# Two norm factors of the last layer's boundary, taken from four sums per token gathered during the output projection

## The chip, the cores and the metric

The kernel runs on one core of a Trainium2 chip. The metric is the device time of one execution in microseconds (us); each kernel is timed in several runs and the median is given. PE is the matmul engine (TensorE), PEld its weight load, DVE the vector engine, ACT the scalar engine, POOL the general engine (GpSimd), SP the engine whose queue issues the DMAs.

## The reference

A sequence of 512 tokens with 1024 features goes through two hybrid layers and then two transformer layers with a context stream. All arithmetic is float32 in its result. The place that matters here is the middle of the last layer, between its attention and its feed-forward part:

```python
def rms_norm_2(x, g):
    xf = x.astype(jnp.float32)
    y = xf * lax.rsqrt(jnp.mean(xf * xf, axis=-1, keepdims=True) + EPS)
    return (y * g.astype(jnp.float32)).astype(x.dtype)
...
        y = ... @ w_out                          # attention, output projection
        x = x + g1 * rms_norm_2(y, norm_g[l, 1])         # first norm: of y
        h = rms_norm_2(x, norm_g[l, 2]) * (1.0 + sc2) + sh2   # second norm: of the new x
        x = x + g2 * rms_norm_2(swiglu(h, ffn_w_in[l], ffn_w_out[l]), norm_g[l, 3])
```

The first norm needs one factor per token, r1 = (mean(y^2) + eps)^-1/2. The second needs r2 = (mean(x'^2) + eps)^-1/2, where x' = x + G*y*r1 and G is the product of the gate g1 and the gain, one number per feature.

## The kernel before

Activations lie feature by feature: a tensor of 1024 features and 512 tokens is eight tiles of 128 partitions (features) by 512 columns (tokens), numbered k or f from 0 to 7. A sum over features is therefore a sum over tiles, and then a matmul with a column of ones (`ones_col`). Every matmul of a weight with an activation is done in three parts on values split in a high and a low half (`hh`, `hl` for the activation, `wh`, `wl` for the weight): high by high, high by low, low by high. The split of a weight tile is a cast on ACT (`weights`, L422) and a subtraction on POOL or, for one weight in three, on DVE (`lo`, L398 and L400). A weight has three buffers for the raw data and two for each half.

The last layer's second stretch runs so:

1. `out_proj` (L970): half of the output projection (features 0 to 3 of its input) was done earlier, beside the attention. Now the other four are added: for each of the eight output tiles f, `dense` loads a weight of 128x512, splits it, and runs 12 matmuls of 512 columns into one PSUM bank (four banks, tags "d" and "b", in turn); `proj` (L616 to L632) adds the bank to y on DVE (L625), ACT squares the sum (L503), and POOL adds the square to a running tile (L631; the last tile's square stays apart). Woven with it, `prepare` loads and splits four weights of the feed-forward part (`u0` to `u3`).
2. `boundary` (L579): the tile of squares and the last square go through the matmul with ones (`rstd_cols`, L389), then a small DVE operation (L481), the power -1/2 on POOL (L483), and four PE transposes that spread the factor over 128 partitions (`spread`, L498). Then `postnorm_tile` for each k: a DVE operation with G and r1 (L576) and an addition to x on POOL (even k) or DVE (odd k, L577). Then the new x is squared tile by tile on ACT (L503), the squares are added on DVE (L515, L518), and the same column sum, power and transposes give r2. Then `norm_tile` for each k (DVE L554, ACT L556 or L560) and the split of h (L557, L398).
3. `outer` runs the first four feed-forward weights, 12 matmuls for each tile k of h, into four banks. After that `ffn` goes on as a plain row of matmuls to the end of the kernel, and a last `boundary` writes the output.

The old x is loaded by two DMAs of 1 MB (L586) and the new x is written back by two (L593), on SP's queue.

The order of instructions on each engine is set when the program is built: a scheduler takes, by a number of priority that follows the order of the code, whatever is ready by its own reckoning. `ahead(n)` shifts that number. In this stretch `stage(low=3, load=800, split=-200, ...)` holds: loads of weights stand 800 places earlier, and splits of weights (ACT cast and POOL or DVE subtraction) 200 places later than where the code has them. On the chip each engine then works strictly in the order written.

Of the kernel before, what the change touches and what calls it, by code (L numbers as in the profile page):

```python
# [11 lines left out]
F32 = mybir.dt.float32  # L12
# [4 lines left out]
AF = mybir.ActivationFunctionType  # L17
ALU = mybir.AluOpType
# [4 lines left out]
D = 1024  # L23
KD = D // 128
S = 512
NT = S // 128
# [3 lines left out]
EPS = 1e-6  # L30
# [169 lines left out]
class Net:  # L200
# [136 lines left out]
    def first(self, g, n):  # L337
        for _ in range(n):
            next(g)
            yield  # L340
# [235 lines left out]
        nc.vector.scalar_tensor_tensor(t, y[k // 4][:, k % 4, :], gain[:, k:k + 1], r, op0=ALU.mult, op1=ALU.mult)  # L576
        (nc.vector if k in [1, 3, 5, 7] else nc.gpsimd).tensor_add(x[:, k, :], x[:, k, :], t)  # L577

    def boundary(self, y, ysq, xsrc, gain, nxt, xdst, early=None):  # L579


        nc = self.nc
        with self.phase("x") as ph:
            x = ph.tile([128, KD, S], F32, name=self.name("x"))
            for i in range(2):
                nc.sync.dma_start(x[:, 4 * i:4 * i + 4], xsrc[:, 4 * i:4 * i + 4])  # L586
            al = partial(self.tl, ph, dt=F32, tag="bp", bufs=8 if early else 5), self.bank if early else self.flat
            yield
            if y is not None:
                yield from self.postnorm_steps(x, y, ysq, S, gain, al)  # L590
            if xdst is not None:
                for i in range(2):
                    nc.sync.dma_start(xdst[:, 4 * i:4 * i + 4], x[:, 4 * i:4 * i + 4])  # L593
            yield
            if nxt is None:
                return None
            h = yield from self.prenorm_steps(x, S, *nxt, al=al)
            if not early:
                return h
            acc = [self.bank([128, S], "d") for _ in range(2)]  # L600
            for _ in range((len(early) - 1) // 2):
                w = self.wide()
                acc += [w[:, 0, :], w[:, 1, :]]
            acc = acc[:len(early)]
            self.outer(early, h, acc)
            yield
            return h, dict(enumerate(acc))

    def outer(self, ws, h, acc, ks=range(KD)):

# [1159 lines left out]
    def run(self):  # L1770
        nc, I = self.nc, self.I
        x1, x2, x3, x4 = (self.scr([128, KD, S], f"x{i}") for i in range(4))
        self.stage(low=3)
        h, ready = self.start()
# [3 lines left out]
        m, mc = (self.mods2(0, ada[0][0][i], "xy"[i]) for i in range(2))  # L1778
        with self.phase("c1") as self.c1:
# [10 lines left out]
            with self.phase("ctx") as ph:  # L1790
                done = {}
                with self.phase("xc") as px:
                    xc = px.tile([128, KD, CL], F32, name="xc0")
                    nc.sync.dma_start(xc, I["ctx"])
                    y, sq = self.weave((self.out_proj(I["w_out"][0], mix[0], S, *mix[1:]), 8, 0),
                                       (self.keep(done, self.prenorm_steps(xc, CL, *mc(0), pool=ph)), 9, 0))
                scc, win, lat = self.even_project(done["result"], CL, 0, False, ph)
                h = self.weave((self.boundary(y, sq, I["x"], self.post_mod1(0), self.pre_mod1(1), x1), 18, 0), (win(), 4.5, -200))
# [9 lines left out]
        with self.phase("c2") as self.c2:  # L1808
# [6 lines left out]
            with self.phase("ctxa") as ph:  # L1815
                at = self.area(ph, "c", kp=1, k=4, q=8, v=3, p=8)
                y, sq = self.weave((self.out_proj(I["w_out"][1], mix[0], S, *mix[1:]), 8, 30),
                                   (self.chain(self.even_ctx_window(at, scc["q"], oc[0]),
                                               self.even_latent(at, scc, CL, CL, oc[1])), 12, 0))
            self.stage(low=3)  # L1820
            with self.phase("ctxo") as ph:
                hc = self.split_o(oc, CL, self.new_h(CL, ph))
                done = {}
                h = self.weave((self.boundary(y, sq, x1, self.post_mod1(1), m(0), x2), 18, 0),
                               (self.keep(done, self.out_proj(I["ev_w_out"], hc, CL)), 8, 0))
# [13 lines left out]
            with self.phase("cf") as cf:  # L1839
# [14 lines left out]
                y, sq = self.result(self.out_proj(I["ev_w_out"], self.split_o(o, S, self.new_h(S)), S))  # L1854
                h = self.weave((self.boundary(y, sq, x2, m(1), m(2), x3), 18, 60), (rest, 14.4, 0))
            g2 = m(3)
            self.stage(low=3)
            m, mc = (self.mods2(1, ada[1][0][i], "xy"[i]) for i in range(2))
            with self.phase("ctx") as cx:
                with self.phase("ffn") as ph:  # L1860
# [3 lines left out]
                    f = self.ffn(0, h, S, hid)  # L1864
# [3 lines left out]
                    y, sq = self.weave((f, 8, 0), (self.keep(done, self.prenorm_steps(xc, CL, *mc(0), pool=cx)), 9, 0))  # L1868
                _, val, diff, keys, _ = self.odd_project(done["result"], CL, 0, False, cx)
                h = self.weave((self.boundary(y, sq, x3, g2, m(0), x4), 18, 0),  # L1870
                               (self.chain(diff(0), keys(), val(0), diff(1), val(1)), 5, 0))
        self.stage(low=3, max=-200, turn=300)
        with self.phase("odd") as ph:
# [4 lines left out]
            ready = {}  # L1878
# [9 lines left out]
            h = self.new_h(S)  # L1888
            self.split_o(o, S, h, range(4))
            y = self.open_y()  # L1890
# [5 lines left out]
        with self.phase("early") as ph:  # L1896
            early = []

            def prepare():
                for u in range(4):  # L1900
                    src = I["ffn_w_in"][1, u % 2 * NFH + u // 2].rearrange("p k c -> p (k c)")
                    early.append(self.weights(src, 1024, (ph, f"u{u}")))
                    yield

            y, sq = self.weave((self.out_proj(I["od_w_out"], h, S, y, range(4)), 8, 0),
                               (prepare(), 4.2, 0))
            h, ready = self.weave((self.boundary(y, sq, x4, m(1), m(2), x1, early), 1, 0))
            self.close_y()
            self.stage(low=3)
            with self.phase("ffn") as ph:  # L1910
                hid = lambda: [self.tl(ph, [128, KD, S], F32R, "hid", 2) for _ in range(2)]
                y, sq = self.result(self.ffn(1, h, S, hid, ready))
# [70 lines left out]
```

## Time and profile before

| | us |
|---|---|
| median of 3 runs | 2823.11 (2820.75 to 2828.60) |
| profiled execution, its own time | 2819.89 |
| span of its profile | 2818.1 |
| PE busy in the span | 2455.0 (87%) |
| DVE, ACT, POOL busy | 1258.7, 1188.2, 1079.4 |
| output projection's second half, last matmul | from 2383.5 to 2412.3 |
| first matmul of the feed-forward part | 2436.16 |
| last matmul of the feed-forward part | 2800.0 |

Times of rows are counted from the span's start. The share of PE is an average over many stages; the change touches one of them, between about 2384 and 2461 us. A row of the time line gives start, duration, engine, line of the code, operation, the tile written and the tiles read, the shape, and how many instructions it merges; in square brackets stands how long the engine was idle before and what ended that.

### The profile page before, as it was taken

How to read it: one execution, taken by the hardware profiler on the slowest of the kernel's cores; microseconds unless marked ns; L12 is line 12 of the kernel's file. 1: busy time of each engine (PE TensorE's matmuls, PEld its weight loads, DVE VectorE, ACT ScalarE, POOL GpSimd, SP SyncE). 2: the span in 40 equal slices, each digit the busy share in tenths (PEclk: the TensorE clock that was granted, in tenths of full speed). 3: DMA queues.
4: the chain of work that ended last, by engine and by line, in shares of the span. 5: the costliest groups of instructions: out<-in, count | busy, mean ns of one | idle time of the engine just before them, and what ended most of it. 6: DMA issues, size and time to landing. Idle time of an engine off the chain costs nothing. (4 is left out here: it accounts for less than half of the span.)

```text
span 2818.1 us, 35394 instructions
## 1 busy us (share of the span) xinstructions
PE 2455.0 (87%) x13052; PEld 1994.9 (71%) x13052; DVE 1258.7 (45%) x2065; ACT 1188.2 (42%) x2227; POOL 1079.4 (38%) x754
## 2 busy tenths in 40 slices
PE   6988896778888886769999899999888989799997
PEld 4765666666666665648998777777776777688886
DVE  3655357235646644445442631212645767421212
ACT  3534365333547534445554522222434646332222
POOL 2435235344533551213455732322542222443334
PEclk9988998888979987879999999999988989899998
DMA  7364644344344652335553545454444253333332
GB/s 244 121 205 156 207 165 154 107 140 162 104 124 139 213 182 100 116 112 143 174 159 135 186 135 172 149 169 133 148 140 158 90 153 113 113 100 97 94 97 75
DMA packets 170816, 400.56 MB, mean 142 GB/s; under 512 B 19378, under 2 KB 60820, under 8 KB 167316
## 3 DMA queue, kind: packets, MB, share of 16 engines
q1 hardware_dynamic: 170644, 398.31, 43.7%
q8 instruction: 103, 1.69, 0.2%
q14 instruction: 69, 0.57, 0.1%
HBM read 339.85 MB, written 58.39 MB: 141 GB/s over the span
## 5 line engine op out<-in xcount | busy, mean ns | idle before, releaser
L398 POOL TENSOR_TENSOR wl<-wr,wh 128x1024 fp32r<-128x1024 f32 (+3 forms) x245 | 538.2, 2198 | 899.5 <-ACT wh L422 451.5
L422 ACT CAST wh<-wr 128x1024 fp32r<-128x1024 f32 (+3 forms) x367 | 353.8, 964 | 706.5 <-PE d L389 279.5
L389 PE MATMUL d<-hh,wh 128*128 128x512 f32 x960 | 398.4, 415 | 19.7 <-ACT hh L556 7.8
L389 PE MATMUL d<-hl,wh 128*128 128x512 f32 x960 | 394.0, 410 | 1.9 <-DVE hl L557 0.9
L389 PE MATMUL d<-hh,wl 128*128 128x512 f32 x960 | 263.5, 403 | 0.0
L400 DVE SCALAR_TENSOR_TENSOR wl<-wr,wh 128x1024 fp32r<-128x1024 f32 (+3 forms) x122 | 152.1, 1246 | 227.8 <-PE d L389 91.9
L389 PEld LDWEIGHTS d<-hh,wh 128*128 128x128 f32 x960 | 190.6, 199 | 62.2 <-ACT hh L556 8.4
L389 PEld LDWEIGHTS d<-hl,wh 128*128 128x128 f32 x960 | 189.7, 198 | 42.5 <-issue 2.5
L389 PEld LDWEIGHTS d<-hh,wl 128*128 128x128 f32 x960 | 185.0, 195 | 39.6 <-issue 1.6
L400 DVE SCALAR_TENSOR_TENSOR pg<-b,pg 128x512 fp32r<-128x512 f32 (+1 forms) x208 | 137.2, 665 | 68.7 <-ACT pg L404 67.2
L389 PE MATMUL b<-hh,wh 128*128 128x512 f32 x416 | 164.2, 395 | 0.0
L389 PE MATMUL b<-hl,wh 128*128 128x512 f32 x416 | 163.2, 392 | 0.0
L934 POOL TENSOR_TENSOR oy<-pg,pg 64x256 f32<-64x256 f32 (+1 forms) x72 | 57.7, 802 | 262.3 <-DVE pg L932 91.3
L404 ACT CAST pg<-b 128x512 fp32r<-128x512 f32 (+1 forms) x208 | 117.1, 570 | 80.2 <-PE b L909 68.2
L882 DVE TENSOR_REDUCE sm<-s 128x1 f32<-128x768 f32 (+3 forms) x144 | 120.7, 846 | 26.6 <-PE s L389 25.9
L389 PE MATMUL d<-hc,wh 128*128 128x256 f32 x656 | 105.4, 311 | 23.7 <-DVE rp L400 11.8
L950 DVE SCALAR_TENSOR_TENSOR rp<-rp,d 128x512 f32<-128x512 f32 (+1 forms) x77 | 46.7, 607 | 165.5 <-ACT rp L949 165.4
L1745 DVE SCALAR_TENSOR_TENSOR rp<-rp,b 128x512 f32<-128x512 f32 (+1 forms) x64 | 38.1, 595 | 175.3 <-PE b L389 174.8
L389 PE MATMUL d<-hid,wh 128*128 128x512 f32 (+1 forms) x528 | 114.7, 361 | 1.5 <-POOL hid L398 1.5
L389 PEld LDWEIGHTS d<-hc,wh 128*128 128x128 f32 x656 | 94.9, 211 | 28.3 <-ACT wh L422 12.2
L389 PE MATMUL b<-hid,wh 128*128 128x512 f32 (+1 forms) x528 | 110.8, 361 | 0.0
L389 PE MATMUL b<-hh,wl 128*128 128x512 f32 x416 | 103.8, 389 | 0.0
(416 smaller groups left out, 5143.2 us busy)
## 6 DMA issues: line engine op xcount, KB each, us to landing
wr<-in_ffn_w_in SPq DMA_DIRECT2D x132, 512.0 KB
mr<-in_ada_w SPq DMA_DIRECT2D x96, 512.0 KB
wr<-in_ffn_w_out SPq DMA_DIRECT2D x48, 512.0 KB
x<-x SPq DMA_DIRECT2D x20, 1024.0 KB
wr<-in_w_in SPq DMA_DIRECT2D x38, 512.0 KB
mr<-in_w_mod SPq DMA_DIRECT2D x32, 512.0 KB
wr<-in_ev_w_in SPq DMA_DIRECT2D x20, 512.0 KB
wr<-in_ffn_w_out SPq DMA_DIRECT2D x24, 384.0 KB
```

Source lines behind the costliest of these rows:

```text
L389: self.nc.tensor.matmul(out, lhsT, rhs, start=start, stop=stop)
L398: self.nc.gpsimd.tensor_sub(out, src, hi)
L400: self.nc.vector.scalar_tensor_tensor(out, src, scale, hi, op0=ALU.mult, op1=ALU.subtract)
L404: self.nc.scalar.copy(hi, src)
L422: nc.scalar.copy(hi[:, :n], raw[:, :n])
L882: nc.vector.reduce_max(c, s, axis=AX.X, negate=True)
L934: nc.gpsimd.tensor_tensor(d, sel(t), sel(rs), op=ALU.mult)
L950: nc.vector.scalar_tensor_tensor(t, t, 1.0, ps, op0=ALU.add, op1=ALU.mult)
L1745: nc.vector.scalar_tensor_tensor(g, g, 0.5, pu, op0=ALU.mult, op1=ALU.mult)
```

## The change

The old x is loaded before the projection (`residual`). During the projection (`joint_proj`) four sums per token are gathered: of y^2, of (G*y)^2, of G*y*x and of x^2. With r1 known, the sum of squares of the new x is r1^2 * sum((Gy)^2) + 2 * r1 * sum(Gyx) + sum(x^2), so r2 follows from six small DVE operations on 128x4 numbers (`joint_boundary`) without a pass over the new x. For tiles 0 to 5 the terms are added tile by tile (squares of y and of Gy on POOL, Gyx and x^2 on DVE); tiles 6 and 7 go straight into the matmul with ones, for the squares with a two-column right side (1 and G^2). The column sums are matmuls on PE into one bank. In `joint_boundary` r1 and r2 are both spread at once, and for each k the new x, the normed h and the matmuls of `outer` follow each other. The new x is written after k = 3 and k = 7. `boundary` loses its `early` branch; its other callers do as before.

```diff
--- before.py
+++ after.py
@@ -576,15 +576,14 @@
         nc.vector.scalar_tensor_tensor(t, y[k // 4][:, k % 4, :], gain[:, k:k + 1], r, op0=ALU.mult, op1=ALU.mult)
         (nc.vector if k in [1, 3, 5, 7] else nc.gpsimd).tensor_add(x[:, k, :], x[:, k, :], t)
-    def boundary(self, y, ysq, xsrc, gain, nxt, xdst, early=None):
-
+    def boundary(self, y, ysq, xsrc, gain, nxt, xdst):
         nc = self.nc
         with self.phase("x") as ph:
             x = ph.tile([128, KD, S], F32, name=self.name("x"))
             for i in range(2):
                 nc.sync.dma_start(x[:, 4 * i:4 * i + 4], xsrc[:, 4 * i:4 * i + 4])
-            al = partial(self.tl, ph, dt=F32, tag="bp", bufs=8 if early else 5), self.bank if early else self.flat
+            al = partial(self.tl, ph, dt=F32, tag="bp", bufs=5), self.flat
             yield
             if y is not None:
                 yield from self.postnorm_steps(x, y, ysq, S, gain, al)
@@ -595,16 +594,109 @@
             if nxt is None:
                 return None
             h = yield from self.prenorm_steps(x, S, *nxt, al=al)
-            if not early:
-                return h
-            acc = [self.bank([128, S], "d") for _ in range(2)]
-            for _ in range((len(early) - 1) // 2):
-                w = self.wide()
-                acc += [w[:, 0, :], w[:, 1, :]]
-            acc = acc[:len(early)]
-            self.outer(early, h, acc)
-            yield
-            return h, dict(enumerate(acc))
+            return h
+    @contextmanager
+    def residual(self, xsrc):
+        with self.phase("x") as ph:
+            x = ph.tile([128, KD, S], F32, name=self.name("x"))
+            for i in range(2):
+                self.nc.sync.dma_start(x[:, 4 * i:4 * i + 4], xsrc[:, 4 * i:4 * i + 4])
+            yield x, (partial(self.tl, ph, dt=F32, tag="bp", bufs=8), self.bank)
+    def joint_proj(self, wsrc, h, y, ks, x, gain, al):
+        nc = self.nc
+        cols = self.flat([128, NT, 4])
+        w2 = self.sm([128, 2, 2])
+        nc.vector.memset(w2, 1.0)
+        nc.vector.tensor_tensor(w2[:, :, 1], gain[:, 6:8], gain[:, 6:8], op=ALU.mult)
+        n = [0]
+        def add(tile, rhs, c, last=False):
+            for t in range(NT):
+                self.mm(cols[:, t, c:c + rhs.shape[-1]], tile[:, t * 128:t * 128 + 128], rhs, n[0] == 0,
+                        last and t == NT - 1)
+                n[0] += 1
+        sums, late = None, []
+        for f in range(KD):
+            ps = self.dense(wsrc[f, :, ks[0]:ks[-1] + 1].rearrange("p k c -> p (k c)"), h, S, ks, "db"[f % 2])
+            dst = y[f // 4][:, f % 4, :]
+            new = al[0] if f == 0 else self.rp
+            g = gain[:, f:f + 1]
+            nc.vector.tensor_add(dst, ps, dst)
+            sq, xz = new([128, S]), new([128, S])
+            nc.scalar.activation(sq, dst, AF.Square)
+            nc.vector.scalar_tensor_tensor(xz, dst, g, x[:, f, :], op0=ALU.mult, op1=ALU.mult)
+            if f < 6:
+                z = new([128, S])
+                nc.scalar.activation(z, dst, AF.Square, scale=g)
+                if f == 0:
+                    sums = sq, z, xz
+                    xx = al[0]([128, S])
+                    nc.scalar.activation(xx, x[:, 0, :], AF.Square)
+                else:
+                    nc.gpsimd.tensor_add(sums[0], sums[0], sq)
+                    nc.gpsimd.tensor_add(sums[1], sums[1], z)
+                    nc.vector.tensor_add(sums[2], sums[2], xz)
+            else:
+                late.append((sq, xz))
+            for k in ((), (1,), (2,), (3,), (4,), (5,), (6, 7), ())[f]:
+                t = self.square(x[:, k, :], S)
+                nc.vector.tensor_add(xx, xx, t)
+            if f == 6:
+                for i, t in enumerate(sums):
+                    add(t, self.ones_col, i)
+            yield
+        add(xx, self.ones_col, 3)
+        for i, (sq, xz) in enumerate(late):
+            add(sq, w2[:, i, :], 0)
+            add(xz, self.ones_col, 2, i == 1)
+        return cols
+    def joint_boundary(self, y, cols, x, al, gain, nxt, xdst, early):
+        nc = self.nc
+        def power(ms):
+            r = self.sm([128, NT, 1])
+            nc.gpsimd.tensor_tensor(r, ms, self.mhalf[:, None, :].to_broadcast([128, NT, 1]), op=ALU.pow)
+            return r
+        ms, q = self.sm([128, NT, 1]), self.sm([128, NT, 1])
+        nc.vector.tensor_scalar(ms, cols[:, :, 0:1], 1.0 / D, EPS, op0=ALU.mult, op1=ALU.add)
+        r1 = power(ms)
+        ms = self.sm([128, NT, 1])
+        nc.vector.tensor_tensor(q, cols[:, :, 1:2], r1, op=ALU.mult)
+        nc.vector.scalar_tensor_tensor(q, cols[:, :, 2:3], 2.0, q, op0=ALU.mult, op1=ALU.add)
+        nc.vector.tensor_tensor(q, q, r1, op=ALU.mult)
+        nc.vector.tensor_tensor(q, cols[:, :, 3:4], q, op=ALU.add)
+        nc.vector.tensor_scalar(q, q, 0.0, None, op0=ALU.max)
+        nc.vector.tensor_scalar(ms, q, 1.0 / D, EPS, op0=ALU.mult, op1=ALU.add)
+        r2 = power(ms)
+        r1, r2 = self.spread(r1, S, al=al), self.spread(r2, S, al=al)
+        h = self.new_h(S)
+        acc = [self.bank([128, S], "d") for _ in range(2)]
+        w = self.wide()
+        acc += [w[:, 0, :], w[:, 1, :]]
+        def first(k):
+            t = al[0]([128, S])
+            nc.vector.scalar_tensor_tensor(t, y[k // 4][:, k % 4, :], gain[:, k:k + 1], r1, op0=ALU.mult, op1=ALU.mult)
+            (nc.gpsimd if k in [2, 4, 6] else nc.vector).tensor_add(x[:, k, :], x[:, k, :], t)
+        first(0)
+        for k in range(KD):
+            if k + 1 < KD:
+                first(k + 1)
+            self.norm_tile(h, x, k, S, r2, *nxt, al)
+            self.outer(early, h, acc, [k])
+            if k % 4 == 3:
+                nc.sync.dma_start(xdst[:, k - 3:k + 1], x[:, k - 3:k + 1])
+        return h, dict(enumerate(acc))
     def outer(self, ws, h, acc, ks=range(KD)):
@@ -1902,9 +1994,10 @@
                     early.append(self.weights(src, 1024, (ph, f"u{u}")))
                     yield
-            y, sq = self.weave((self.out_proj(I["od_w_out"], h, S, y, range(4)), 8, 0),
-                               (prepare(), 4.2, 0))
-            h, ready = self.weave((self.boundary(y, sq, x4, m(1), m(2), x1, early), 1, 0))
+            with self.residual(x4) as (x, al):
+                cols = self.weave((self.joint_proj(I["od_w_out"], h, y, range(4, 8), x, m(1), al), 8, 0),
+                                  (prepare(), 4.2, 0))
+                h, ready = self.joint_boundary(y, cols, x, al, m(1), m(2), x1, early)
             self.close_y()
             self.stage(low=3)
             with self.phase("ffn") as ph:
```

## Rows read from the trace of the kernel before

**Rows 1.** Busy time by stretch: us, then each engine's busy time, clock, DMA.
```profile
core 0: us, PE busy (x) PEld busy (x) DVE busy (x) ACT busy (x) POOL busy (x), PEclk, DMA share, GB/s
2400.00:2414.00 14.00, 13.06 (x62) 10.62 (x60) 6.73 (x7) 8.52 (x12) 13.75 (x10) 1.00 0.61 181
2420.00:2435.00 15.00, 2.96 (x12) 2.50 (x12) 10.60 (x18) 4.32 (x8) 5.70 (x4) 0.50 0.34 140
2435.00:2450.00 15.00, 13.84 (x51) 11.03 (x52) 8.82 (x12) 7.92 (x12) 5.21 (x4) 0.81 0.00 0
2740.00:2760.00 20.00, 20.00 (x90) 16.57 (x89) 3.81 (x5) 5.72 (x7) 9.09 (x5) 1.00 0.26 75
```

**Rows 2.** Time line of PE from 2384 to 2442 us.
```profile
2384.76 0.40 PE L389 MATMUL d<-hl,wh 128*128 128x512 f32 x1
...
2390.82 0.63 PE L389 MATMUL b<-hl,wh 128*128 128x512 f32 x1
...
2411.27 1.07 PE L389 MATMUL b<-hh,wl 128*128 128x512 f32 x4
2413.28 1.95 PE L389 MATMUL b<-blk,rp 128*128 128x1 f32 x16 [0.94 <-POOL rp L631]
...
2430.26 1.84 PE L389 MATMUL b<-blk,bp 128*128 128x1 f32 x8 [12.70 <-DVE bp L518]
2433.45 1.12 PE L498 MATMUL b<-ident,sm 128*128 128x128 f32 x4 [1.35 <-POOL sm L483]
2436.16 0.79 PE L389 MATMUL d<-hh,u0h 128*128 128x512 f32 x1 [1.60 <-ACT hh L556]
```

**Rows 3.** Time line of DVE, from the projection's end to the second norm.
```profile
2410.27 1.82 DVE L400 SCALAR_TENSOR_TENSOR wl<-wr,wh 128x1024 fp32r<-128x1024 f32 x1
2412.38 0.69 DVE L625 TENSOR_TENSOR y<-b,y 128x512 f32<-128x512 f32 x1 [0.29 <-PE b L389]
2415.26 0.16 DVE L481 TENSOR_SCALAR sm<-b 128x4 f32<-128x4 f32 x1 [2.19 <-PE b L389]
2417.60 2.06 DVE L576 SCALAR_TENSOR_TENSOR bp<-oy,x,b 128x512 f32<-128x512 f32 x3 [2.17 <-PE b L498]
2419.58 0.68 DVE L577 TENSOR_TENSOR x<-x,bp 128x512 f32<-128x512 f32 x1
...
2425.70 3.69 DVE L515 TENSOR_TENSOR bp<-bp,bp 128x512 f32<-128x512 f32 x6
...
2434.60 2.06 DVE L554 SCALAR_TENSOR_TENSOR bp<-x,x,b 128x512 f32<-128x512 f32 x3 [2.31 <-PE b L498]
```

**Rows 4.** Time line of ACT: the last square of y, the first tile of h.
```profile
2413.10 0.63 ACT L503 ACTIVATE rp<-y 128x512 f32<-128x512 f32 x1 [0.46 <-DVE y L625]
...
2435.39 0.72 ACT L556 ACTIVATE hh<-bp,ada 128x512 fp32r<-128x512 f32 x1 [8.46 <-DVE bp L554]
```

**Rows 5.** Time line of POOL in the projection and the first norm.
```profile
2395.29 2.55 POOL L398 TENSOR_TENSOR wl<-wr,wh 128x512 fp32r<-128x512 f32 x2 [5.86 <-PE b L389]
2397.79 1.29 POOL L631 TENSOR_TENSOR rp<-rp,rp 128x512 f32<-128x512 f32 x1
...
2403.88 2.13 POOL L631 TENSOR_TENSOR rp<-rp,rp 128x512 f32<-128x512 f32 x1
...
2409.73 3.50 POOL L631 TENSOR_TENSOR rp<-rp,rp 128x512 f32<-128x512 f32 x2
...
2415.50 1.02 POOL L483 TENSOR_TENSOR sm<-sm,mhalf 128x4 f32<-128x4 f32 x1
2418.42 2.96 POOL L577 TENSOR_TENSOR x<-x,bp 128x512 f32<-128x512 f32 x2 [1.90 <-DVE bp L576]
```

**Rows 6.** SP's queue: the new x is written, the next load of x.
```profile
2422.25 3.92 SPq L593 DMA_DIRECT2D x<-x  x2
2460.40 0.80 SPq L586 DMA_DIRECT2D x<-x  x2
```

## The prediction

> **What bounds the kernel now.** I read the table of busy time by stretch first. From the feed-forward part on, PE is busy in 20.00 of 20 us at the full clock (one slice of it stands in [rows 1], the others are like it). So whatever moves the first feed-forward matmul moves the end of the kernel by the same amount, and the question is only when that matmul starts. The same table shows two different stretches ahead of it. From 2400 to 2414 us, the output projection, PE has 13.06 of 14 us and POOL 13.75: both are full, DVE has half its time free. From 2420 to 2435 us PE has 2.96 of 15 us and its clock has fallen to 0.50, the lower level of 1.2 GHz: that is the boundary, where DVE and small steps bound it.
>
> The time line of PE gives the marks [rows 2]. The last projection matmuls start at 2411.27 and end at 2412.3. The column sum of squares is done at 2413.28 + 1.95 = 2415.23; I call this moment C. The first feed-forward matmul starts at 2436.16, so C to there is 20.93 us. Between lie eight new tiles of x, the second pass of squares that ends with six DVE additions of 3.69 us [rows 3], its own column sum of 1.84 us and transposes of 1.12 us [rows 2].
>
> **What the change takes off behind C.** After it, C is the moment when all four sums stand, and then follow, each waiting for the one before: a small DVE operation, 0.03 us of handing over and 0.16 [rows 3]; the power on POOL, 0.08 + 1.02 [rows 5]; six small DVE operations; a second power, 1.10; four transposes, 0.05 + 1.12 [rows 2]; the first normed tile on DVE, 0.03 + 0.74 (three take 2.06 when queued) [rows 3]; ACT, 0.05 + 0.72 [rows 4]; PE, 0.05. The six are shown nowhere as a chain. Six times 0.16 is 0.96, with 0.09 of gap each 1.5; I take 1.25, near the lower because that row is the same size. Sum: 0.19 + 1.10 + 1.25 + 1.10 + 1.17 + 0.77 + 0.77 + 0.05 = 6.4 us. The r1 spread is beside it. Behind it DVE makes two tiles of new x, 0.69 + 0.68 each, so it can be up to 0.6 us late for the normed tile. I take 6.7, bounds 6.3 and 7.3. Gain: 20.93 - 6.7 = 14.2 us.
>
> Behind the first matmul nothing new becomes the bound. Per pair of tiles DVE then has two operations of 0.69 with r1, two with r2, one addition and one split, about 4.2 us, while PE takes 24 matmuls; 90 take 20.00 us at full clock [rows 1], so 24 take 5.3. PE starts at the lower clock as it does now (0.79 and 0.63 a matmul, clock 0.81 over that stretch) [rows 1, 2]; I count no change there. The two writes of x move from 2422 to some 2440 and 2450; behind them on SP's queue stands first the load of 2460.40 [rows 6], so they delay nothing. The loads of the old x only stand earlier in the code; they still wait for their space, and I count nothing (bounds 0 and 1 us).
>
> **What it costs before C.** First PE. Four sums over eight tiles (three running tiles, the x^2 tile, two times two late ones) replace two, and 16 column-sum instructions for two tiles took 1.95 us, 0.98 a tile [rows 2]; at the lower clock it is 1.84. Were PE alone the limit, the projection would end where it does and C would be 2412.3 + 8 x 0.98 = 2420.1, 4.9 us later than now.
>
> Then POOL and DVE. Now POOL does one split and one addition a tile. For tiles 1 to 5 it gets a second addition, and DVE three operations that it has not now, all reading two tiles of SBUF: the product with x, its addition, the addition of x^2. The rows show that such a DVE operation and a POOL operation never run together. POOL's addition at 2409.73 is followed at once by another, 3.50 us for two where two splits took 2.55 [rows 5]; the DVE split that came in at 2410.27 and lasted 1.82 [rows 3] first stood until POOL's first was done (about 2411.0) and then held up the second for 1.1. In the first norm POOL's operation began at 2418.42 and is over at 2419.7 by the usual 1.29; the DVE addition of 2419.58 ends at 2420.26, 0.55 later, and POOL's pair lasts 2.96 instead of 2.55 [rows 3, 5]. So one share has to be split: POOL 1.25 (2.55 / 2 less the overlap of issuing) for an operation of 512 columns, DVE 0.55.
>
> From 2395.29, when POOL's first free weight buffer lets it start [rows 5], up to the last addition on POOL (of tile 5), that share must hold: on POOL five splits and ten additions, 15 x 1.25 = 18.75; on DVE six products, five additions of them and five of x^2, 16 x 0.55 = 8.8. Together 27.55, so 2422.8. A weight split on DVE in this stretch (1.1) and two of the x^2 additions done before it starts (2 x 0.55) cancel. Then PE still has seven tiles of sums to run, 7 x 0.98 = 6.9, beside which the last projection tile's steps fit. C = 2429.7, that is 14.5 us later than now. Bounds: 4.9 (PE alone) and, if the last splits of weights come after the additions and PE has then to do tile 7 as well, about 18.5.
>
> The rule of the Trainium skill that bears on this, "SBUF — State Buffer", section "Who interferes with whom", is that a DVE instruction with two SBUF inputs and a GpSimd one that reads SBUF take an exclusive lock, the loser blocked for the whole instruction. The exclusion agrees with the rows; the whole length does not quite, since 0.55 of the 0.68 us showed. By whole instructions the sum would be 16 x 0.13 = 2.1 us longer.
>
> The sum: 14.5 - 14.2 = +0.3 us, no change that can be seen. The profiled execution took 2819.89, so 2820.2 of that kind; the median of the runs shown is 3.2 us above it, so 2823.4. I say 2823.
>
> **The rivals.** (1) PE stays the limit: 4.9 - 14.2 = -9.3 us, 2814. For it: ACT and DVE sit idle for some us before 2395, when x is already there, and x^2 work could go there; PE has four banks to run ahead. Against it: ten additions and five splits on POOL alone end at 2414, and with the eleven DVE operations that need y at 2420, and seven tiles of sums still follow; it takes work that I put on one share to run side by side after all. 17%.
>
> (2) Slower, through the clock. PE now has to wait for weight splits that stand behind POOL's additions. The splits have the lower priority, so additions that are ready go first: tile 5's split comes after three others and six additions, 2395.29 + 10 x 1.25 + 8 x 0.55 = 2412.2, while PE can have done its high parts some five us earlier. After 2384.76 PE had only a column sum and transposes for five us, and its next matmuls took 0.63 instead of 0.39 to 0.40 [rows 2], the lower level. If it falls so and the seven sums after the last addition run at 1.84 instead of 0.98, that is 7 x 0.86 = +6.0, in all +6.3: 2829. It decides once PE waits about as long as there (2385.2 to 2390.2, 5 us) near 2415 to 2420. For it: 2395.3 to 2422.8 is 27.5 us, and PE has some 17 us of matmuls in it. Against it: the waits come as several shorter ones, and the split of a tile can come before the additions. 16%.
>
> **How the numbers follow.** The forecast has 67%, with its own range of 4 us either way (C between 10.5 and 18.5 late). The range takes in most of the rivals: 2813 to 2830. I call 0.3%, 8.5 us, what a measurement of this kernel can tell from no change. Faster by more: half of rival 1 and a little of the forecast, 14%. Slower by more: half of rival 2, and the late splits together with the lower clock, 12%. Within: 74%.
>
> **What would show it.** In the profile after: the last POOL addition of tile 5 near 2423, POOL and DVE operations there lengthened to 1.7 and over 1 us; PE with waits for a split (POOL) between 2403 and 2420; four sums done near 2430; the first feed-forward matmul 6 to 7 us after that, near 2436 to 2437; then PE full to the end. The prediction is wrong if POOL's additions end before 2418 (rival 1), if the column sums take 1.8 us a tile (rival 2), or if the stretch behind C takes over 8 us.

## The result, and the profile after

The changed kernel took 2841.05 us (median of 4 runs, 2837.29 to 2844.20), the kernel before 2825.23 beside it (4 runs): a ratio of 1.0064, 95% interval 1.0044 to 1.0084. It is slower by some 16 us where I forecast no change, and outside my range of 2813 to 2830.

Single executions of either kernel lie up to 24 us apart (2807.5 to 2831.6 in 23 of the kernel before), and most of that arises ahead of the change: in the profile after, the stage starts 7 us later than in the one of before, and 6.9 of them stand already at an operation of the attention 19 us earlier (2375.51 and 2382.44). So I compare inside one profile, from a fixed mark: the start of DVE's addition of tile 0. Before, then after:

```profile
2394.90 0.69 DVE L625 TENSOR_TENSOR oy<-d,oy 128x512 f32<-128x512 f32 x1
```

```profile
2401.86 0.69 DVE L630 TENSOR_TENSOR oy<-d,oy 128x512 f32<-128x512 f32 x1
```

I call the time from there to the first feed-forward matmul the stage. It was 41.26 us and is 58.14, 16.9 us longer. From there to the end it was 381.9 us and is 382.4. All of the loss is in the stage.

PE's time line after answers to [rows 2]. (Start, duration, engine, line, operation, tiles, shape, count, idle before.)

```profile
2415.04 1.20 PE L389 MATMUL b<-hh,wl 128*128 128x512 f32 x4 [0.36 <-POOL wl L398]
2420.24 0.79 PE L389 MATMUL d<-hh,wh 128*128 128x512 f32 x1 [4.00 <-ACT wh L422]
2420.83 0.63 PE L389 MATMUL d<-hl,wh 128*128 128x512 f32 x1
...
2428.55 1.87 PE L389 MATMUL s<-blk,bp 128*128 128x1 f32 x8 [3.86 <-POOL bp L642]
2430.28 0.77 PE L389 MATMUL b<-hh,wh 128*128 128x512 f32 x1
...
2431.70 3.41 PE L389 MATMUL s<-blk,bp 128*128 128x1 f32 x16
2434.97 0.77 PE L389 MATMUL b<-hl,wh 128*128 128x512 f32 x1
...
2437.25 1.91 PE L389 MATMUL b<-hh,wl 128*128 128x512 f32 x4
2442.24 1.87 PE L389 MATMUL s<-blk,bp 128*128 128x1 f32 x8 [3.08 <-DVE bp L649]
...
2449.09 1.85 PE L389 MATMUL s<-blk,rp 128*128 128x1 f32 x8
2452.28 1.12 PE L498 MATMUL b<-ident,sm 128*128 128x128 f32 x4 [1.35 <-POOL sm L666]
2457.29 1.12 PE L498 MATMUL b<-ident,sm 128*128 128x128 f32 x4 [3.89 <-POOL sm L666]
2460.00 0.79 PE L389 MATMUL d<-hh,u0h 128*128 128x512 f32 x1 [1.59 <-ACT hh L556]
```

Read from the top: PE waits 4.00 us before tile 6, whose matmuls then go at the lower clock (0.63 for 0.39). It waits 3.86 us for the first running tile. The eight instructions of that tile's sum stand in PE's order ahead of tile 7, three of whose matmuls follow; then come 16 more for the other two running tiles, and only then the rest of tile 7. It is done at 2439.16, 37.3 us after the mark; before it was 17.4. Then PE waits 3.08 us for a DVE addition, and five sums of 1.71 us each (start to start, 1.85 long) end at 2450.94. That is C, 49.08 us after the mark.

Both waits lead back to DVE. These are rows of ACT, of DVE and of POOL:

```profile
2417.92 0.63 ACT L632 ACTIVATE rp<-y 128x512 f32<-128x512 f32 x1 [2.42 <-DVE y L630]
...
2419.59 1.12 ACT L422 CAST wh<-wr 128x512 fp32r<-128x512 f32 x2
```

```profile
2425.56 0.68 DVE L630 TENSOR_TENSOR y<-b,y 128x512 f32<-128x512 f32 x1
```

```profile
2427.04 1.45 POOL L642 TENSOR_TENSOR bp<-bp,rp 128x512 f32<-128x512 f32 x1 [1.96 <-ACT rp L632]
```

The wait before tile 6 ends with its weight cast on ACT, and that stands behind the squares of tile 4, which waited for DVE's addition of tile 4. The wait for the first running tile ends with an addition for which POOL itself stood idle for 1.96 us: PE had tile 5 ready at 2416.24, but DVE added it only at 2425.56.

POOL's time line answers to [rows 5]: operations of 1.29 have become 1.71 to 1.74, and the last addition of tile 5 ends at 2430.17, 28.31 us after the mark.

```profile
2413.25 1.74 POOL L398 TENSOR_TENSOR wl<-wr,wh 128x512 fp32r<-128x512 f32 x1
2414.96 1.72 POOL L642 TENSOR_TENSOR bp<-bp,rp 128x512 f32<-128x512 f32 x1
...
2428.46 1.71 POOL L643 TENSOR_TENSOR bp<-bp,rp 128x512 f32<-128x512 f32 x1
2439.29 2.34 POOL L398 TENSOR_TENSOR wl<-wr,wh 128x1024 fp32r<-128x1024 f32 x1 [9.13 <-PE b L389]
...
2455.80 1.43 POOL L666 TENSOR_TENSOR sm<-sm,mhalf 128x4 f32<-128x4 f32 x1 [3.57 <-DVE sm L678]
```

DVE's time line answers to [rows 3]. The x^2 addition of tile 7 stands behind tile 7's own addition and then meets a weight split on POOL (2.38 us for 0.68). In the last rows the six small operations for r2 (L673 to L678) take 3.46 us in all, since operations that make new x (L688, L689) stand between them.

```profile
2412.67 1.17 DVE L644 TENSOR_TENSOR bp<-bp,rp 128x512 f32<-128x512 f32 x1
2413.76 1.78 DVE L649 TENSOR_TENSOR bp<-bp,rp 128x512 f32<-128x512 f32 x1
...
2439.19 0.69 DVE L630 TENSOR_TENSOR y<-b,y 128x512 f32<-128x512 f32 x1 [4.75 <-PE b L389]
2439.80 2.38 DVE L649 TENSOR_TENSOR bp<-bp,rp 128x512 f32<-128x512 f32 x1
...
2450.97 0.16 DVE L670 TENSOR_SCALAR sm<-s 128x4 f32<-128x4 f32 x1 [8.12 <-PE s L389]
...
2452.26 0.16 DVE L673 TENSOR_TENSOR sm<-s,sm 128x4 f32<-128x4 f32 x1 [1.13 <-POOL sm L666]
...
2453.44 0.75 DVE L688 SCALAR_TENSOR_TENSOR bp<-oy,x,b 128x512 f32<-128x512 f32 x1 [0.62 <-PE b L498]
2454.10 0.15 DVE L676 TENSOR_TENSOR sm<-s,sm 128x4 f32<-128x4 f32 x1
...
2455.56 0.16 DVE L678 TENSOR_SCALAR sm<-sm 128x4 f32<-128x4 f32 x1
```

Busy time by stretch answers to [rows 1]; the last three numbers are PE's clock, the DMA share and the GB/s.

```profile
2415.00:2420.00 5.00, 1.20 (x4) 0.67 (x4) 5.00 (x5) 2.58 (x5) 4.66 (x4) 0.99 0.15 52
...
2445.00:2450.00 5.00, 5.00 (x25) 5.00 (x25) 0.00 (x0) 0.00 (x0) 0.00 (x0) 0.50 0.00 0
```

### The profile page after: what moved, and what is told of

Same layout as the page of the kernel before. It is cut to its first block, busy times and chain, and to the rows that moved or that the text cites. A ratio compares the mean times of both kernels' runs of the same rounds, so it can differ in the third digit from the quotient of the medians.

```text
span 2842.4 us, 35501 instructions
## 1 busy us (share of the span) xinstructions
PE 2470.3 (87%) x13092; PEld 2007.8 (71%) x13092; DVE 1285.1 (45%) x2086; ACT 1189.9 (42%) x2233; POOL 1087.8 (38%) x757
## 5 line engine op out<-in xcount | busy, mean ns | idle before, releaser
L389 PEld LDWEIGHTS d<-hh,wh 128*128 128x128 f32 x960 | 190.4, 198 | 69.0 <-ACT wh L422 13.8
L974 DVE TENSOR_REDUCE sm<-s 128x1 f32<-128x768 f32 (+3 forms) x144 | 120.8, 846 | 27.3 <-PE s L389 26.8
L389 PE MATMUL d<-hc,wh 128*128 128x256 f32 x656 | 105.9, 312 | 24.2 <-DVE rp L400 12.4
L389 PEld LDWEIGHTS d<-hc,wh 128*128 128x128 f32 x656 | 95.5, 212 | 28.5 <-ACT wh L422 11.9
```

The costliest lines, as they stand in the source:

```text
L389: self.nc.tensor.matmul(out, lhsT, rhs, start=start, stop=stop)
L974: nc.vector.reduce_max(c, s, axis=AX.X, negate=True)
```

## The experiments

All times of the table are from each kernel's own profile, in us after its mark. There is one profile of each, but where two kernels share a stretch it comes out alike: the sums are ready at 49.08 in the changed kernel and at 49.07 in gather_only.

| kernel | tile 7 done | sums ready | first feed-forward matmul (the stage) |
|---|---|---|---|
| before | 17.4 | 20.3 (y^2 alone) | 41.26 |
| after | 37.3 | 49.1 | 58.14 |
| tail_only | 17.4 | 20.8 (y^2 alone) | 29.87 |
| gather_only | 37.3 | 49.1 | 70.07 |
| sums_last | 25.5 | 44.4 | 53.45 |
| adds_dve | 17.4 | 39.8 | 49.04 |
| warm | 18.0 | 40.2 | 50.40 |
| warm_late | 18.0 | 40.8 | 50.99 |
| dve_x2 | 17.8 | 39.6 | 49.77 |
| psum_acc | 24.2 | 46.0 | 53.27 |
| rows | 21.9 | 27.3 | 36.44 |
| rows_q | 22.0 | 27.6 | 35.63 |
| rows_r | 21.9 | 27.3 | 34.35 |

**Each half alone.** In tail_only the gathering of three sums is taken out, in gather_only the short way behind the sums.

```diff
 # tail_only
...  # z, xz, xx, their additions and their column sums are left out
-  nc.vector.tensor_tensor(q, cols[:, :, 1:2], r1, op=ALU.mult)   # and columns 2, 3
+  nc.vector.tensor_tensor(q, cols[:, :, 0:1], r1, op=ALU.mult)
 # gather_only, behind the four sums
+  r1 = self.spread(power(ms), S, al=al)
+  for k in range(KD):
+      self.postnorm_tile(x, y, k, S, r1, gain, al)
...
+  h = self.run_through(self.prenorm_steps(x, S, *nxt, al=al))
```

> Left out: the sums of (Gy)^2, Gyx and x^2; the column of y^2 is read in place of all four, gathered as in the kernel before. What remains of the change is the short way behind the sums. The stage is measured from DVE's first addition of tile 0 to the first feed-forward matmul: 41.26 us before, 58.14 after. If gain and cost add up (in the changed kernel the way behind the sums takes 9.06 us instead of 20.93), the stage is 41.26 - 11.87 = 29.4 and the kernel some 12 us faster than before. If the way behind the sums was long only because PE's clock was low or because of what the gathering left queued there, it is the 6.7 us of the prediction, 27.0.

> The four sums are gathered as in the changed kernel, but only y^2 is used; behind them stands the boundary of the kernel before with its second pass. If the cost lies in the gathering (sums done 28.75 us later than before, by each kernel's own first addition), the stage is 41.26 + 28.75 = 70.0, and with the other half (29.4) the two add up to the change. If the low clock or the order behind the sums made a part of it, it is nearer to 60.

Measured: 29.87 and 70.07. Against 41.26 that is -11.39 and +28.81, together +17.4; the change has +16.88. Gain and cost add up to 0.5 us. The kernel times of these single runs (2813.96 and 2850.92, 2828.11 for before beside them) point the same way, -14.2 and +22.8, but single executions lie too far apart to tell the sizes. The way behind the sums is 9.05 us in tail_only too, where nothing of the gathering is queued there: my 6.7 was too small by itself.

**The order of PE's work.**

```diff
-            if f == 6:
-                for i, t in enumerate(sums):
-                    add(t, self.ones_col, i)
             yield
+        for i, t in enumerate(sums):
+            add(t, self.ones_col, i)
         add(xx, self.ones_col, 3)
```

> The changed kernel with one step moved: the column sums of the three running tiles stand behind tile 7's matmuls in the code, not ahead of them. Theory queue (PE's written order holds tile 7 back behind sums that wait for POOL): tile 7 runs some 11 us earlier and the stage falls from 58.1 to about 46. Theory share (POOL and DVE can't both read SBUF, and POOL's last addition sets the end): POOL's last addition stays at 28.3 us after the stage's start, eight column sums and 9 us follow, so it falls less, to 50 to 52, the sums still at the lower clock.

Measured: 53.45. Tile 7 is done 11.8 us earlier, as the queue theory has it, but the stage falls by 4.7 only. POOL's last addition stays at 28.29, and behind the three sums PE waits for the last x^2 addition and then runs five sums at the lower clock:

```profile
2432.51 1.05 PE L389 MATMUL s<-blk,bp 128*128 128x1 f32 x8 [1.13 <-POOL bp L642]
2434.19 3.57 PE L389 MATMUL s<-blk,bp 128*128 128x1 f32 x16 [0.62 <-POOL bp L643]
2441.55 1.86 PE L389 MATMUL s<-blk,bp 128*128 128x1 f32 x8 [3.79 <-DVE bp L649]
```

So neither theory had the size: the order is worth 4.7 us, less than the 12 of one and than the 6 to 8 of the other. What comes last now is DVE's own queue: PE has tile 7 ready at 2431.39, but DVE adds it only at 2438.33, and the last x^2 addition stands behind that.

**Who adds.** In the changed kernel, POOL's ten additions on DVE; PE's sums then stand behind tile 7 in the written order, as in sums_last.

```diff
-                    nc.gpsimd.tensor_add(sums[0], sums[0], sq)
-                    nc.gpsimd.tensor_add(sums[1], sums[1], z)
+                    nc.vector.tensor_add(sums[0], sums[0], sq)
+                    nc.vector.tensor_add(sums[1], sums[1], z)
```

> The changed kernel with POOL's ten additions on DVE. In the written order PE's column sums then stand behind tile 7 by themselves, so it is to be compared with the run before it, sums_last. Theory share: ten operations of 1.25 us become ten of 0.55 in the share that only one of the two engines can use, splits come through sooner, the last addition comes up to 7 us earlier and the stage is 3 to 7 us shorter than in sums_last. Theory load (DVE is simply full: 18.6 us of work in the projection, and 6 more): DVE is the limit and the stage is 3 us longer than in sums_last or more.

Measured: 49.04, 4.4 us less than sums_last, in the range of the share theory and against the load theory. With only splits on POOL, PE isn't held up at all: tile 7 is done at 17.4, as before the change. Then it stands idle for 8.15 us, since DVE now is behind, and all eight sums run at the lower clock (5.28 us for the first three):

```profile
2425.33 5.28 PE L389 MATMUL s<-blk,bp 128*128 128x1 f32 x24 [8.15 <-DVE bp L642]
```

The last of the ten additions ends at 26.1 us, 2.2 earlier than on POOL, of up to 7 expected. DVE is the limit here as well, but alone it is sooner done than the two engines in turns.

**Where the operand lies.** In sums_last, the running tile of Gyx in PSUM.

```diff
-            sq, xz = new([128, S]), new([128, S])
+            sq, xz = new([128, S]), bank[:, 1, :] if f == 0 else new([128, S])
...
+        gx = self.rp([128, S])
+        nc.scalar.copy(gx, sums[2])
```

> sums_last with one operand moved: the running tile of Gyx lies in a PSUM bank and not in SBUF, so that its five DVE additions read one SBUF tile instead of two; the count of operations on every engine stays (one ACT copy more behind the last). Theory share (what excludes POOL is a DVE operation that reads two tiles of SBUF): these five run while POOL runs, in 0.7 us each, and POOL's last addition ends 5 x 0.55 = 2.8 us earlier, at 25.5 us after the stage's start instead of 28.3; the stage gets 2 to 3 us shorter. Theory load (POOL's operations of 1.7 us are so long for another reason, such as DVE being busy at all): POOL's last addition stays at 28.

Measured: POOL's last addition ends at 27.05 instead of 28.29, and the stage is 53.27 instead of 53.45. The five additions run beside POOL's operations in 0.68 to 0.70 us, while the x^2 additions next to them, with both operands in SBUF, wait. DVE's time line of psum_acc, then POOL's:

```profile
2405.86 0.68 DVE L645 TENSOR_TENSOR s<-s,rp 128x512 f32<-128x512 f32 x1
2406.46 1.81 DVE L650 TENSOR_TENSOR bp<-bp,rp 128x512 f32<-128x512 f32 x1
...
2414.53 2.28 DVE L400 SCALAR_TENSOR_TENSOR u3l<-wr,u3h 128x1024 fp32r<-128x1024 f32 x1
```

```profile
2404.75 1.72 POOL L398 TENSOR_TENSOR wl<-wr,wh 128x512 fp32r<-128x512 f32 x1
...
2415.69 2.27 POOL L644 TENSOR_TENSOR bp<-bp,rp 128x512 f32<-128x512 f32 x1
...
2421.47 2.24 POOL L644 TENSOR_TENSOR bp<-bp,rp 128x512 f32<-128x512 f32 x1
```

That it is the operand's place that excludes POOL is shown by these durations. The Trainium skill, "SBUF — State Buffer", section "Who interferes with whom", states that a DVE instruction with at most one SBUF input, outside the 2-port perf modes, does not contend with GpSimd; the trace agrees, by the 0.68 to 0.70 us above. The forecast end (25.5) was missed by 1.5 us: two weight splits of 1024 columns on DVE now fall beside POOL's additions, which took 2.27 and 2.24 us there instead of 1.29, about 1.9 more in all. The stage gained nothing, because C came 1.6 us later than in sums_last: PE's sums waited for the copy of the PSUM tile on ACT, which stood behind tile 7's square, and all eight then ran at the lower clock.

```profile
2428.89 3.54 PE L389 MATMUL s<-blk,bp 128*128 128x1 f32 x16 [8.00 <-ACT rp L653]
```

The way behind C, 7.26 us instead of 9.06, took that back: here five of the six small operations stand on DVE ahead of the first new x.

**The clock.** In warm 36 matmuls should have filled PE's idle time in adds_dve, in warm_late nine float32 matmuls on y.

```diff
 # warm
+        for i in range(36):
+            self.mm(bank[:, 1, :], warm[0][0][:, i % 8 * 128:i % 8 * 128 + 128], h[0][:, i % 8, :], i == 0, i == 35)
 # warm_late
+        for i in range(9):
+            self.mm(bank[:, 1, :], y[1][:, 0, :128], y[1][:, 0, :], i == 0, i == 8)
```

> adds_dve with 36 matmuls of 512 columns more, into a bank that nobody reads, behind tile 7's and ahead of the column sums: PE stood idle there for 8.2 us, and they take 36 x 0.227 = 8.2 at the full clock. Theory clock (PE's idle time lowers its clock, and each of the eight column sums then takes 1.72 us from start to start instead of 0.98): the sums run at the full clock and the stage goes from 49.0 to about 42.5, though PE does more. If the sums were slow for another reason (their inputs come late, one by one), it stays at 49 or grows.

> adds_dve with nine float32 matmuls of 512 columns on y's tile 4, into a bank that nobody reads, written in PE's order between tile 7 and the column sums, where PE stood idle for 8.2 us; I count 0.85 us each, 7.7 in all. Theory clock: the eight column sums run at 0.98 us each instead of 1.72, and the stage goes from 49.0 to 43, though PE does more. Rival (the sums are slow by themselves or wait for their inputs): 49 or more.

Measured: 50.40 and 50.99, no gain from either, although the three sums right behind the added matmuls did get faster. In warm 27 of the 36 run where PE stood idle (the scheduler put nine of them further ahead), in warm_late all nine, as 18 instructions. PE's time lines, first of warm, then of warm_late:

```profile
2420.52 6.46 PE L389 MATMUL s<-hh,u0h 128*128 128x512 f32 x27
2428.68 3.16 PE L389 MATMUL s<-blk,bp 128*128 128x1 f32 x24 [1.69 <-DVE bp L643]
2434.26 1.87 PE L389 MATMUL s<-blk,bp 128*128 128x1 f32 x8 [2.42 <-DVE bp L650]
```

```profile
2420.98 7.99 PE L389 MATMUL s<-y 128*128 128x512 f32 x18 [0.90 <-DVE y L631]
2428.81 2.73 PE L389 MATMUL s<-blk,bp 128*128 128x1 f32 x24
2434.20 1.87 PE L389 MATMUL s<-blk,bp 128*128 128x1 f32 x8 [2.66 <-DVE bp L650]
```

The three sums behind them take 3.16 and 2.73 us instead of 5.28: in warm_late 0.91 each, with a granted clock of 1.00 from 2428.80 to 2431.60. Then PE waits 2.42 and 2.66 us for DVE's last x^2 addition, and the five sums behind that are at the lower clock again. So a column sum takes nearly twice as long at the lower clock, and the sums were slow for that reason; but the saved time ends in the wait for DVE, whose last x^2 addition comes 0.4 and 1.0 us later than in adds_dve. In the changed kernel, sums_last, adds_dve, warm and warm_late alike, C comes 8.7 to 8.8 us behind the end of that addition: five sums at the lower clock. No run here has faster sums behind that addition, so what the clock costs the stage is not shown by itself. I expected 43 because I took the eight sums for one block.

**The x^2 additions earlier.** In adds_dve:

```diff
+        for k in range(1, KD):
+            t = self.square(x[:, k, :], S)
+            nc.vector.tensor_add(xx, xx, t)
         sums, late = None, []
```

> adds_dve with the sum of x^2 made ahead of the projection in the code; four or five of its seven DVE additions then stand before or at the first projection tiles. Theory load (in adds_dve DVE is the limit, busy from the first tile to tile 7): the stage is shorter by what DVE is relieved of in it, two to five times 0.6 us, 46 to 48. Theory clock alone: PE waits and loses its clock all the same, the sums' 14 us stay, and the stage is 48 to 49.

Measured: 49.77, a little more than adds_dve. Eight sums wait for nothing between them here and still take 13.8 us, at the lower clock, after an idle stretch of 7.96 us. It was a miss for the load theory, and for the clock it is 0.8 more than expected. C came 0.2 us earlier than in adds_dve, and the way behind it took 10.2 us instead of 9.2. Four of the seven x^2 additions stand inside the stage after all: DVE added tile 5 1.4 us later than in adds_dve, and tiles 6 and 7 only 0.4 earlier.

**No additions.** In rows the sums come from fast matmuls of 512 columns (operands rounded as for the weight matmuls, the type fp32r of the profile); rows_q and rows_r change the order behind the sums.

```diff
 # rows
+            self.mm(acc, pick[:, i, :], tile, n[0] == 0, n[0] == 3 * KD - 1)   # acc: 4 x 512
...
+            last = self.rp([128, S], F32R), self.rp([128, S], F32R)
+            nc.scalar.activation(last[0], dst, AF.Square)
+            nc.vector.scalar_tensor_tensor(last[1], dst, gain[:, f:f + 1], x[:, f, :], op0=ALU.mult, op1=ALU.mult)
...
+            self.mm(cols[:, t, :], rows[:, t * 128:t * 128 + 128], self.ident[:4, :4], t == 0, t == NT - 1)
 # rows_q, in joint_boundary
+        nc.vector.scalar_tensor_tensor(hold, ms, 0.0, r1, op0=ALU.mult, op1=ALU.add)
+        r1, r2 = self.spread(hold, S, al=al), self.spread(r2, S, al=al)
 # rows_r
+            self.norm_tile(h, x, k, S, r2, *nxt, al)
             if k + 1 < KD:
                 first(k + 1)
-            self.norm_tile(h, x, k, S, r2, *nxt, al)
```

> No additions on POOL or DVE at all: squares of y, of x and the products Gyx are written rounded as operands of the fast matmul, and 24 matmuls of 512 columns with a four-column weight (1 and G^2; 1; 1) add the four sums as rows of one bank, 0.227 us each; then one copy and four small matmuls turn them to columns. Theory share: with one DVE operation a tile (the product) beside POOL's one split, splits are in time, PE is not held up, and the stage is 17.4 + 16 to 24 x 0.227 + 1.5 + 1.7 + 9.1 = 33 to 35, some 7 us less than before the change. Rival: PE's own added work or the first tiles' inputs hold it, and it is not below 41.

> rows with r1 spread only after the small operations for r2 (they stood behind two tiles of new x on DVE in the changed kernel, 9.06 us from the sums to the first feed-forward matmul). If DVE's written order made that stretch 2.3 us longer than predicted, the stage is 2 us shorter than in rows; if the small operations and the powers are just slower than I counted, it is the same or longer by the one operation added.

> rows_q with the normed tile k ahead of the new x of tile k + 1 in the code. In rows_q DVE makes two tiles of new x (2.5 us) between r2 and the first normed tile. If that is what the stretch behind the sums still waits for, the stage is 1.2 us shorter than the 35.6 of rows_q, 34.4, and the kernel 5 to 6 us faster than before, which is just what five rounds may tell; if r2 comes last, it is the same.

Measured, stage: 36.44, 35.63 and 34.35, that is 4.8, 5.6 and 6.9 us below the kernel before. For rows I had expected 33 to 35: tile 7 is done at 21.9, as the added matmuls let one expect, but behind it DVE's last product took 2.44 us instead of 0.75 beside a weight split on POOL. Ahead of the mark these three lose 1.1 us (from the result of the attention's third head to the mark 20.5 us instead of 19.4), since x is squared there. The kernel's time against before, five rounds each: 0.9995 (0.9980 to 1.0010), 0.9988 (0.9974 to 1.0002) and 0.9980 (0.9967 to 0.9993). The last is clear of 1: 2820.09 against 2826.14 us in the medians. POOL's splits in rows_r are back at 1.29 to 1.30 us while they meet no addition:

```profile
2411.83 1.30 POOL L398 TENSOR_TENSOR wl<-wr,wh 128x512 fp32r<-128x512 f32 x1 [3.07 <-ACT wh L422]
```

From the first small operation to the first feed-forward matmul rows takes 9.0, rows_q 7.9, rows_r 7.0 us. Putting the small operations together took 1.1 us off this way and 0.8 off the stage, of the 2 expected; the order of the tiles took 0.9 off the way and 1.3 off the stage (1.2 expected). In DVE's time line of rows_r one stands behind the other without a gap, and the first new x and the first normed tile follow:

```profile
2429.81 0.16 DVE L662 TENSOR_SCALAR sm<-s 128x4 f32<-128x4 f32 x1 [2.27 <-PE s L389]
...
2432.09 0.17 DVE L670 TENSOR_SCALAR sm<-sm 128x4 f32<-128x4 f32 x1
...
2433.66 0.75 DVE L682 SCALAR_TENSOR_TENSOR bp<-oy,x,b 128x512 f32<-128x512 f32 x1 [1.21 <-PE b L498]
2434.44 0.69 DVE L683 TENSOR_TENSOR x<-x,bp 128x512 f32<-128x512 f32 x1
2435.23 0.75 DVE L554 SCALAR_TENSOR_TENSOR bp<-x,x,b 128x512 f32<-128x512 f32 x1
```

## Why the prediction was wrong

- *What bounds the kernel, and that the stage passes on whole.* Right: 0.5 us between the profiles from the first feed-forward matmul to the end.
- *POOL and DVE take turns, and POOL's last addition comes at 2422.8*, 27.9 us after the mark. It came at 28.31. That the two take turns is right: psum_acc shows that the operand's place is the cause, and adds_dve what the turns cost PE. The end is in part luck. POOL ran six splits where I counted five (1.25 us), and it stood idle for 2.8 us where I had it full; against that, its sixteen operations were lengthened by 5.2 us in all where I counted 8.8. A full turn of one operation each took 1.70 us, so DVE's share was 0.45 and not 0.55.
- *Then seven sums, 6.9 us, beside which the last projection tile's steps fit.* This is the step that failed: from POOL's last addition to C it took 20.8 us, 13.9 more. PE's time line divides them. The seven sums took 12.0 us, 5.1 more, at 1.71 us each instead of 0.98: the lower clock, my rival 2, which I had put at 6.0 with 1.84 us a sum. It came as I had said, behind waits of PE (4.00 and 3.86 us, somewhat shorter than the 5 that I had named). The matmuls of tile 7 took 5.7 us between the sums, at the lower clock too, and not beside them: the written order put tile 7 behind sums that waited for POOL. I had named this as a bound (18.5 instead of 14.5, so 4.0) and left it out of the sum. And PE waited 3.1 us for the last x^2 addition, which stands on DVE behind tile 7's addition and is held up by a weight split on POOL; this I did not see. The three can't be taken off one by one: sums_last, which mends the order, gained 4.7 us, since DVE's last x^2 addition then came last.
- *The way behind C, 6.7 us (bounds 6.3 and 7.3).* Wrong by 2.4: 9.06, in tail_only too. I put the six small operations in a row, 1.25 us, and the tiles of new x beside them. The scheduler wrote them in turns on DVE, where one tile waited for the r1 transposes: 3.46 us. The second power took 1.43 us instead of 1.02, with one of DVE's additions to x beside it. With both orders mended the way is 7.0 from the first small operation.
- *The gain of 14.2 us* was then 11.9, and the cost of 14.5 was 28.8: 28.8 - 11.9 = 16.9. Two of the signs that I had named for being wrong were there: sums of 1.7 to 1.8 us a tile, and a way behind C of over 8 us.
- *The range.* Its upper end left room for one bad case, the clock or the late tile 7. Both came with PE's waits for the running tiles, so they came together; I had added them up only as a part of a chance of 12%.
- *Rival 1* (PE stays the limit) is out for the change. rows_r goes a part of that way: with no additions the stage is 6.9 us shorter than before, where the rival had 9.3.

## What to carry to other kernels

Work that is put beside a full stretch is not free because an engine there is half idle: count POOL's operations and those of DVE that read two tiles of SBUF as one queue, and then ask which waits of PE they lengthen. Where PE has to wait for as long as here, price the steps behind the wait at the lower clock, and look for what the written order puts between. Sums over features were cheapest here as matmuls with few output rows and many columns, with no additions at all.

## What the runs showed of the hardware that I had not expected

Column sums did not raise the clock: from 2445 to 2450 us of the changed kernel PE is busy 5.00 of 5 us with them, and the granted clock stays at 0.50; in warm_late it was at the full level for the three sums behind nine long matmuls. A POOL operation that waits for DVE is lengthened by less than DVE's operation lasts: 1.71 to 1.74 instead of 1.29, with DVE's at 0.68 alone.
